# A hybrid attention layer on one core: denominators spread through DRAM, gate products on GpSimd, more copies on ScalarE

## The chip, the cores and the metric

One Trainium2 chip, of which the kernel uses one core. The metric is the device time of one execution in microseconds (us); lower is better. The core has a matrix engine (TensorE, in the profile PE, its weight loads PEld), VectorE (DVE), ScalarE (ACT), GpSimd (POOL) and SyncE (SP), which only issues DMAs here.

## The reference, cut to what matters

A decoder layer over 2048 tokens of width 1024: `h = rmsnorm(x)`, one input projection, two token mixers side by side, their gated outputs concatenated, an output projection, and the residual added. The change touches the first mixer, eight heads of 64 columns. Each of its heads is a mixture of three dilated windows:

```python
for window, dilation in ((128, 1), (512, 4), (2048, 16)):
    o, m, den = dilated_pattern(q, k, v, rel_bias, window, dilation)
    outs.append(o); log_dens.append(m + jnp.log(den))
alpha = jax.nn.softmax(jnp.stack(log_dens, axis=0), axis=0)
o_a = jnp.sum(alpha[..., None] * jnp.stack(outs, axis=0), axis=0)
mixed = jnp.concatenate([o_a * jax.nn.silu(z_a), o_b * jax.nn.silu(z_b)], axis=-1)
```

The kernel takes one maximum per query over the three windows, adds the three unnormalised outputs, and multiplies once by one over the summed denominators and once by the gate. The second mixer is a latent attention with eight heads.

## The kernel before

The kernel runs in stages. Up to about 670 us it projects the input in tiles and stores q, k, v and the gates in DRAM. From 672 to about 1012 us it works on the eight dilated heads, from 1012 to about 1540 us on the eight latent heads, and after that on the output projection.

**A dilated head.** `seq_s` makes the scores of a head in 24 tiles: `s_tile` (L883) for windows 1 and 2, `s_tile3` (L910) for window 3, each a few matmuls into a PSUM tile `S`, which DVE reduces with the bias (L895, L919). Windows 2 and 3 read regrouped copies of q that POOL casts in `q_turn` (L826, L828) into four rotating buffers. `m_fwd` and `m_back` combine the maxima over the windows: DVE expands them against a constant (L926, L933), PE folds the result. `seq_p` then takes the exponentials on ACT (L1016), turns 128x128 blocks of probabilities on PE into a PSUM tile `T` of three buffers (L1027, L1031), copies `T` to SBUF (`a_evac`, L1040 on DVE or L1042 on ACT, chosen by the tuple `EVA`, here two of four on each), multiplies with v (L1054, L1065) and adds up `acc` (L1076 on ACT, L1080 on DVE). The scores of head h+1 are woven into the second part of head h.

**The tail of a head.** `tail(h)` is woven into the next head's `seq_p`, one item every second step. `a_shift` moves the lower half of `acc` to 64 partitions by a DMA into `bot` (L1107) and loads the gate `g` (L1109). `a_den0` to `a_den2` sum the denominators to `rden`, 128 queries by 16 blocks, and take the reciprocal (L1102). The outputs lie the other way, 64 columns on partitions and 2048 queries along them, so the reciprocals must lie along the free axis, the same on all 64 partitions. `a_out` gets this by PE: four transposes of one broadcast column each into a `T` tile (L1116). Then `a_out2`, one step later, multiplies the gate with it on DVE (L1124), adds the two halves of the output (L1126, on POOL, in the last head on DVE), and multiplies by the gate on POOL (L1127). Four such rounds `m` make a head, 512 queries each; `a_store` writes `bot` to `mixD` (L1130).

**The latent heads** do the same thing another way (`b_den1`, `b_out`): PE turns a [128,4] tile of reciprocals once (L1397), DVE copies it to SBUF (L1399), SP writes it to the DRAM tile `rD` (L1401) and reads it back on 64 partitions with a source stride of 0 (L1403); POOL multiplies (L1418, L1419). `rD` has 16 entries, of which the latent heads use 8 to 15.

**What sets the order.** The program is traced in the order of the Python code, and a planner arranges each engine's instructions ahead of the run by its own model of their times; what it puts on one engine's queue is then executed in that order, each instruction waiting for its semaphores. In the latent stage alone PE's order is as written. All loads and most stores of both attention stages are issued by SP, also one queue in order. After the last dilated head, `tail(7)` is woven with the first score blocks of the latent heads (`b_blocks_s(0, 1)`), whose reductions (L1341) and copies (L1364) run on DVE; the first turned block of the latent stage is partly cleared by POOL (L1368) before the first product with its v (L1379).

Of the kernel before, what the change touches and what calls it, by code (L numbers as in the profile page):

```python
# [21 lines left out]
F32 = mybir.dt.float32  # L22
# [3 lines left out]
OP = mybir.AluOpType  # L26
# [25 lines left out]
NPA = 6  # L52
WPL = (1,)
MXB = 10
EVA = (0, 0, 1, 1)
EVB = (0, 1)
SCALE_B = 96.0 ** -0.5
QA0, KA0, VA0, ZA0, CQ0, CKV0, KR0, ZB0 = 0, 512, 1024, 1536, 2048, 2304, 2432, 2464
# [39 lines left out]
def hybrid_kernel(ctx: ExitStack, tc: tile.TileContext, x, positions, rel_bias, norm_gain, w_in,  # L98
                  a_q_gain, a_k_gain, q_c_gain, w_uq, kv_c_gain, w_ukv, qn_gain, qr_gain,
                  kn_gain, kr_gain, w_out, cmat, ctri, conehot, cinv, out, dbg=None):  # L100
    nc = tc.nc
    pe, dve, act, pool, sp = nc.tensor, nc.vector, nc.scalar, nc.gpsimd, nc.sync
# [26 lines left out]
    rD = [dr.tile([16, 128], F32, name=f"rD{i}") for i in range(16)]  # L129
# [3 lines left out]
    ident = CM[:, 0:128]  # L133
# [543 lines left out]
    for gi, (half, nm) in enumerate(seq):  # L677
# [18 lines left out]
        for i, unit in enumerate(units):  # L696
# [8 lines left out]
            if nm == "g0" and half == 1:  # L705
                b = 12 + i
# [46 lines left out]
            if nm == "g1":  # L753
                b = 8 * half + i
                todo_bg += [("q", b, clock[0]), ("k", b, clock[0] + 4)]
            credit = min(credit + RATE[half] * (1.5 if nm[0] == "z" else 1.0), 1.5)
            if credit >= 1 and todo_bg and todo_bg[0][2] <= clock[0]:
                credit -= 1
                kind, b, _ = todo_bg.pop(0)
# [8 lines left out]
    while todo_bg:  # L768
        kind, b, _ = todo_bg.pop(0)
# [33 lines left out]
    psS = pool_of("pss", "left", PSUM)  # L803
    PA2 = psO = None
    HD = [dict() for _ in range(8)]
# [298 lines left out]
    def a_shift(h):  # L1104
# [3 lines left out]
        H["g"] = PA2.tile([64, S], F32, name="gA_", bufs=1)  # L1108
        sp.dma_start(H["g"], GD[h // 2][64 * (h % 2):64 * (h % 2) + 64, :])  # L1109

    def a_out(h, m):
        H = HD[h]
        s = slice(512 * m, 512 * m + 512)
        tp = psS.tile([128, 4, 128], F32, name="T", bufs=3)
        for i in range(4):
            pe.transpose(tp[:, i, :], H["rden"][:, 4 * m + i:4 * m + i + 1].to_broadcast([128, 128]), ident)  # L1116
        H["tp", "out"] = tp

    def a_out2(h, m):
        H = HD[h]  # L1120
        s = slice(512 * m, 512 * m + 512)
        tp = H["tp", "out"]
        g = H["g"][:, s]
        dve.tensor_tensor(g, tp[0:64].rearrange("p a b -> p (a b)"), g, op=OP.mult)  # L1124
        o = H["bot"][:, s]
        (dve if h == 7 else pool).tensor_tensor(o, H["acc"][0:64, s], o, op=OP.add)  # L1126
        pool.tensor_tensor(o, o, g, op=OP.mult)  # L1127

    def a_store(h):
        sp.dma_start(mixD[h], HD[h]["bot"])  # L1130
# [64 lines left out]

    def tail(h):
        out = [lambda: (a_shift(h), a_den0(h)), lambda: a_den1(h), lambda: a_den2(h)]
        for m in range(5):
            out.append(lambda m=m: (a_out2(h, m - 1) if m else None, a_out(h, m) if m < 4 else None))
        return out + [idle, lambda: a_store(h)]  # L1200

    def lead(h, n):
        fs = seq_s(h)
# [15 lines left out]
    PA2 = pool_of("pa2", "right")  # L1219
# [337 lines left out]
    for b in range(4, 16):  # L1557
        c, o = divmod(b, 4)
# [67 lines left out]
```

## Time and profile before

| | us |
|---|---|
| median of 3 runs | 1735.38 |
| the three runs | 1735.31, 1738.95, 1735.38 |
| the profiled execution | 1730.76 |
| its span, first to last instruction | 1728.9 |

The profiled execution is another one than the three, 4.62 us below their median, and 1.86 us of it lie outside the span. "Busy" is the time in which an engine had an instruction running; matmuls are pipelined, so that their lengths overlap, and the start of the next instruction tells more of what one costs than its length. In a list of groups "idle" is the time in which the engine stood still just before the group's instructions, with what it waited for behind the arrow. A stretch is given in us from the span's start. An average over the span hides that the stages have different limits; the table by stretch below separates them.

### The profile page before, as it was taken

How to read it: one execution, taken by the hardware profiler on the slowest of the kernel's cores; microseconds unless marked ns; L12 is line 12 of the kernel's file. 1: busy time of each engine (PE TensorE's matmuls, PEld its weight loads, DVE VectorE, ACT ScalarE, POOL GpSimd, SP SyncE). 2: the span in 40 equal slices, each digit the busy share in tenths (PEclk: the TensorE clock that was granted, in tenths of full speed). 3: DMA queues.
4: the chain of work that ended last, by engine and by line, in shares of the span. 5: the costliest groups of instructions: out<-in, count | busy, mean ns of one | idle time of the engine just before them, and what ended most of it. 6: DMA issues, size and time to landing. Idle time of an engine off the chain costs nothing.

```text
span 1728.9 us, 29212 instructions
## 1 busy us (share of the span) xinstructions
PE 1650.1 (95%) x10118; PEld 1305.3 (75%) x10118; DVE 990.1 (57%) x2965; ACT 830.0 (48%) x2231; POOL 661.2 (38%) x671
## 2 busy tenths in 40 slices
PE   6999999989999889989999989999999999999998
PEld 5999899889999778777777665566565566557887
DVE  4655555155676134578888776666666666624331
ACT  5655545166566214267777735555555555520000
POOL 2454343016575011054444768266266251311000
PEclk9999999999999989989999999999999999999999
DMA  7356544542556575468774551231231220227642
GB/s 161 90 150 163 143 133 132 186 117 70 130 138 181 182 185 138 110 140 190 183 172 119 133 111 61 60 83 34 56 83 42 48 65 25 71 61 180 187 132 69
DMA packets 222600, 203.76 MB, mean 118 GB/s; under 512 B 102317, under 2 KB 188985, under 8 KB 216308
## 3 DMA queue, kind: packets, MB, share of 16 engines
q1 hardware_dynamic: 136852, 153.85, 35.3%
q10 hardware_dynamic: 85600, 48.04, 10.1%
q8 instruction: 80, 1.31, 0.3%
q14 instruction: 68, 0.56, 0.1%
HBM read 136.45 MB, written 72.20 MB: 121 GB/s over the span
## 4 chain that ended last, share of the span: by engine, by line
PE 75%; DMA 10%; DVE 6%; ACT 4%; issue 2%; POOL 2%; SPq 1%; ACTq 0%; DVEq 0%; POOLq 0%
PE O L1379 8%; PE T L1361 7%; PE mz L229 5%; PE mz L227 5%; PE mz L228 5%; PE O L1065 4%; PE S L883 3%; PE T L1027 3%; PE S L1336 3%; PE S L1338 3%; PE S L1337 3%; PE po L227 3%; PE po L229 3%; PE po L228 3%; PE S L910 2%; PE mm L229 2%
## 5 line engine op out<-in xcount | busy, mean ns | idle before, releaser
L1379 PE MATMUL O<-ptB,VB 128*64 128x512 f32 (+3 forms) x640 | 176.2, 560 | 19.7 <-ACT ptB L1366 18.4
L227 PE MATMUL mz<-wh,hTh 128*128 128x256 f32 (+2 forms) x600 | 182.6, 305 | 0.9 <-ACT hTh L221 0.7
L229 PE MATMUL mz<-wh,hTl 128*128 128x256 f32 (+2 forms) x600 | 178.4, 297 | 2.0 <-DVE hTl L222 2.0
L228 PE MATMUL mz<-wl,hTh 128*128 128x256 f32 (+2 forms) x600 | 177.8, 296 | 0.0
L1364 DVE COPY ptB<-T 128x512 f32<-128x512 f32 (+3 forms) x160 | 97.6, 610 | 126.6 <-PE T L1361 119.8
L1354 ACT ACTIVATE P<-P,msB 128x1024 f32<-128x1024 f32 (+4 forms) x104 | 109.7, 1055 | 125.5 <-DVE msB L1341 124.6
L270 DVE SCALAR_TENSOR_TENSOR wl<-wraw,ng,wh 128x256 fp32r<-128x256 f32 (+2 forms) x176 | 83.5, 512 | 113.6 <-ACT wh L269 110.9
L1336 PE MATMUL S<-kBh,qBh 96*128 96x512 f32 (+2 forms) x320 | 131.0, 409 | 5.5 <-DVE msB L1341 5.4
L1366 ACT ACTIVATE ptB<-T 128x512 f32<-128x512 f32 (+3 forms) x160 | 84.2, 526 | 108.0 <-PE T L1361 107.4
L1361 PEld LDWEIGHTS T<-CM,P 128*128 128x128 f32 x740 | 81.4, 143 | 69.2 <-issue 67.9
L227 PEld LDWEIGHTS mz<-wh,hTh 128*128 128x128 f32 x600 | 115.4, 192 | 3.2 <-ACT hTh L221 2.0
L229 PEld LDWEIGHTS mz<-wh,hTl 128*128 128x128 f32 x600 | 115.4, 192 | 2.7 <-DVE hTl L222 2.7
L1337 PE MATMUL S<-kBl,qBh 96*128 96x512 f32 (+2 forms) x320 | 116.8, 365 | 0.0
L1338 PE MATMUL S<-kBh,qBl 96*128 96x512 f32 (+2 forms) x320 | 116.7, 366 | 0.0
L228 PEld LDWEIGHTS mz<-wl,hTh 128*128 128x128 f32 x600 | 115.6, 193 | 0.1
L143 POOL TENSOR_TENSOR pst<-pst,CM 128x8 f32<-128x8 f32 x48 | 80.2, 1684 | 81.4 <-DVE pst L594 72.8
L269 ACT ACTIVATE wh<-wraw,ng 128x256 fp32r<-128x256 f32 (+2 forms) x168 | 76.6, 514 | 64.0 <-DMA wraw<-in_w_in_dram 26.0
L1361 PE MATMUL T<-CM,P 128*128 128x128 f32 x740 | 105.4, 285 | 0.0
L227 PE MATMUL po<-woh,mh 128*128 128x512 f32 x256 | 101.4, 397 | 1.6 <-ACT woh L1242 1.0
L228 PE MATMUL po<-wol,mh 128*128 128x512 f32 x256 | 101.0, 395 | 1.9 <-POOL wol L1243 1.9
L229 PE MATMUL po<-woh,ml 128*128 128x512 f32 x256 | 101.0, 395 | 0.0
L1379 PEld LDWEIGHTS O<-ptB,VB 128*64 128x64 f32 x640 | 38.8, 135 | 77.5 <-ACT ptB L1366 33.1
(489 smaller groups left out, 4607.8 us busy)
## 6 DMA issues: line engine op xcount, KB each, us to landing
wraw<-in_w_in_dram SPq DMA_DIRECT2D x72, 256.0 KB
V<-vA SPq DMA_DIRECT2D x24, 512.0 KB
xt<-in_x_dram SPq DMA_DIRECT2D x16, 512.0 KB
GD<-zst ACTq DMA_DIRECT2D x32, 256.0 KB
vA<-vA SPq DMA_DIRECT2D x8, 1024.0 KB
Q<-qT SPq DMA_DIRECT2D x8, 1024.0 KB
KH<-kT SPq DMA_DIRECT2D x16, 512.0 KB
KL<-kT SPq DMA_DIRECT2D x16, 512.0 KB
```

The costliest lines, as they stand in the source:

```text
L227: pe.matmul(ps, lh, rh, start=first, stop=False)
L228: pe.matmul(ps, lh, rl, start=False, stop=False)
L229: pe.matmul(ps, ll, rh, start=False, stop=last)
L270: dve.scalar_tensor_tensor(WL[key][:, k, :w], r[:, j, :w], ng[:, k:k + 1], f32(wh), op0=OP.mult, op1=OP.subtract)
L1336: pe.matmul(ps[:, :nm], H["q", "h"][:, q], H["k", "h"][:, k], start=True, stop=False)
L1337: pe.matmul(ps[:, :nm], H["q", "h"][:, q], H["k", "l"][:, k], start=False, stop=False)
L1338: pe.matmul(ps[:, :nm], H["q", "l"][:, q], H["k", "h"][:, k], start=False, stop=True)
L1354: act.activation(t, t, AF.Exp, bias=b, scale=-1.0, accum_out=H["den", c][:, i, d:d + 1])
L1361: pe.transpose(tp[:, d, :], p_part(h, c, d, 128 * j, 128), ident)
L1364: dve.tensor_copy(pt[:, d0:, :], tp[:, d0:, :])
L1366: act.activation(pt[:, d0:, :], tp[:, d0:, :], AF.Copy)
L1379: pe.matmul(o[64 * e:64 * e + 64, d0:, :], V[:, j + e, :], pt[:, d0:, :], start=(j == 0), stop=(j == 4 * c + 2), skip_group_check=True)
```

## The change

The tuple `EVA` goes from two of four copies on ACT to three of four. `a_rd0` turns the whole [128,16] tile of reciprocals with one transpose, copies the [16,128] result to SBUF on DVE, and writes it to `rD[h]` in DRAM. `a_rd1` reads 512 of these values back on 64 partitions into `rbA`, which has one buffer; the read for round m+1 is issued behind round m. `a_out` is now all of a round: the sum of the halves, the gate times `rbA` on POOL, and the product of both on POOL. `a_out2` goes, and the tail has nine items instead of ten.

```diff
-EVA = (0, 0, 1, 1)
+EVA = (0, 0, 0, 1)
...
+    def a_rd0(h):
+
+        tp = psS.tile([128, 4, 128], F32, name="T", bufs=3)
+        pe.transpose(tp[0:16, 0, :], HD[h]["rden"], ident)
+        rt = PA2.tile([16, 128], F32, name="rtA", bufs=1)
+        dve.tensor_copy(rt, tp[0:16, 0, :])
+        sp.dma_start(rD[h], rt)
+
+    def a_rd1(h, m):
+
+        rb = HD[h]["rb", m] = PA2.tile([64, 512], F32, name="rbA", bufs=1)
+        dst = rD[h][4 * m:4 * m + 4, :]
+        sp.dma_start(rb, bass.AP(tensor=dst.tensor, offset=dst.offset, ap=[[0, 64], [1, 512]]))
+
     def a_out(h, m):
         H = HD[h]
         s = slice(512 * m, 512 * m + 512)
-        tp = psS.tile([128, 4, 128], F32, name="T", bufs=3)
-        for i in range(4):
-            pe.transpose(tp[:, i, :], H["rden"][:, 4 * m + i:4 * m + i + 1].to_broadcast([128, 128]), ident)
-        H["tp", "out"] = tp
-
-    def a_out2(h, m):
-        H = HD[h]
-        s = slice(512 * m, 512 * m + 512)
-        tp = H["tp", "out"]
-        g = H["g"][:, s]
-        dve.tensor_tensor(g, tp[0:64].rearrange("p a b -> p (a b)"), g, op=OP.mult)
-        o = H["bot"][:, s]
+        o, g = H["bot"][:, s], H["g"][:, s]
         (dve if h == 7 else pool).tensor_tensor(o, H["acc"][0:64, s], o, op=OP.add)
+        pool.tensor_tensor(g, H["rb", m], g, op=OP.mult)
         pool.tensor_tensor(o, o, g, op=OP.mult)
+        if m < 3:
+            a_rd1(h, m + 1)
...
     def tail(h):
         out = [lambda: (a_shift(h), a_den0(h)), lambda: a_den1(h), lambda: a_den2(h)]
-        for m in range(5):
-            out.append(lambda m=m: (a_out2(h, m - 1) if m else None, a_out(h, m) if m < 4 else None))
-        return out + [idle, lambda: a_store(h)]
+        out.append(lambda: (a_rd0(h), a_rd1(h, 0)))
+        for m in range(4):
+            out.append(lambda m=m: a_out(h, m))
+        return out + [lambda: a_store(h)]
```

## Rows read from the trace of the kernel before

**Rows 1.** The page, part 1: busy time of each engine.
```profile
PE 1650.1 (95%) x10118; PEld 1305.3 (75%) x10118; DVE 990.1 (57%) x2965; ACT 830.0 (48%) x2231; POOL 661.2 (38%) x671
```

**Rows 2.** Busy time by stretch: stage of heads, parts of it, its end.
```profile
core 0: us, PE busy (x) PEld busy (x) DVE busy (x) ACT busy (x) POOL busy (x), PEclk, DMA share, GB/s
744.00:1012.00 268.00, 260.20 (x2052) 200.60 (x2052) 215.12 (x876) 188.49 (x661) 138.12 (x144) 0.99 0.68 153
820.00:838.00 18.00, 18.00 (x147) 14.15 (x146) 15.22 (x74) 18.00 (x67) 2.87 (x5) 1.00 0.81 175
838.00:844.00 6.00, 6.00 (x49) 5.12 (x49) 5.87 (x29) 0.75 (x3) 6.00 (x6) 1.00 0.60 221
...
1012.00:1020.00 8.00, 2.51 (x10) 1.60 (x9) 7.34 (x14) 0.81 (x1) 6.38 (x6) 0.80 0.00 0
```

**Rows 3.** PE in order of time, inside one head (start, length, instruction).
```profile
835.78 0.60 PE L1116 MATMUL T<-CM,rden 128*128 128x128 f32 x4
836.22 0.60 PE L1027 MATMUL T<-CM,Pr 128*128 128x128 f32 x4
```

**Rows 4.** Instructions of L1116 (ns min/median/max, first and last start).
```profile
L1116 PE MATMUL T<-CM,rden x128: 270/273/421, 755.6 to 1012.1; 128*128 128x128 f32 x128
```

**Rows 5.** L1399, which copies turned denominators in the latent heads.
```profile
L1399 DVE COPY rtB<-T x31: 247/269/273, 1026.3 to 1502.3; 4x128 f32<-4x128 f32 x31
```

**Rows 6.** Copies out of PSUM tile T, by engine.
```profile
L1040 DVE COPY PT<-T x80: 539/678/693, 701.7 to 1001.0; 128x512 f32<-128x512 f32 x56, 128x384 f32<-128x384 f32 x24
L1042 ACT ACTIVATE PT<-T x80: 468/592/609, 702.2 to 1002.2; 128x512 f32<-128x512 f32 x64, 128x384 f32<-128x384 f32 x16
```

**Rows 7.** Groups by line and shape, 744 to 1012 (busy, mean, idle).
```profile
L1126 POOL TENSOR_TENSOR bot<-acc,bot 64x512 f32<-64x512 f32 x28 | 34.8, 1271 | 10.6 <-DMA bot<-acc 9.7 <-DVE gA__10110 L1124 0.9
...
L926 DVE TENSOR_TENSOR E<-mc,CM 128x128 f32<-128x128 f32 x6 | 6.8, 1135 | 0.2
...
L1124 DVE TENSOR_TENSOR gA__10110<-T,gA__10110 64x512 f32<-64x512 f32 x4 | 2.7, 678 | 0.5 <-PE T L1116 0.5
...
L926 DVE TENSOR_TENSOR E<-m,CM 128x128 f32<-128x128 f32 x6 | 1.7, 291 | 0.7 <-PE S L1091 0.5
```

**Rows 8.** Who waited for whom, 744 to 1012 (us, times, longest).
```profile
POOL Q L826 <- PE S L883: 61.2, 11, 11.1
...
POOL bot L1126 <- DMA bot<-acc: 9.7, 3, 7.7
...
PE S L910 <- POOL Q L828: 4.0, 1, 4.0
...
PE T L1027 <- DVE PT L1040: 2.6, 3, 1.6
```

**Rows 9.** SP in order of time, through one head's tail.
```profile
855.39 0.54 SPq L1130 DMA_DIRECT2D mixD<-bot  x1
...
869.45 0.50 SPq L1107 DMA_DIRECT2D bot<-acc  x1
```

**Rows 10.** SP in the latent stage: a wait group, one pair in time.
```profile
SPq L1403 <- DMA rD<-rtB: 46.3, 27, 5.2
...
1110.33 0.25 SPq L1401 DMA_DIRECT2D rD<-rtB  x1
1111.56 0.45 SPq L1403 DMA_DIRECT2D rbB<-rD  x1
```

**Rows 11.** The stage's end in order of time: DVE, PE, POOL.
```profile
1012.81 4.62 DVE L1126 TENSOR_TENSOR bot<-acc,bot 64x512 f32<-64x512 f32 x4 [0.39 <-issue]
...
1017.44 0.65 DVE L1124 TENSOR_TENSOR gA__12563<-T,gA__12563 64x512 f32<-64x512 f32 x1
...
1018.81 0.80 PE L1336 MATMUL S<-kBh,qBh 96*128 96x512 f32 x1 [5.38 <-DVE msB L1341]
...
1024.46 1.08 PE L1379 MATMUL O<-ptB,VB 128*64 128x512 f32 x4
...
1019.74 0.20 POOL L1368 MEMSET ptB<- 128x128 f32 x1
```

## The prediction

> **What bounds the kernel now.** I began with the busy times of the whole span [rows 1]: PE works 95% of it, DVE 57%, ACT 48%, POOL 38%. That is an average over stages, so the second view is the table by stretch [rows 2], over the stretch in which the tails of the dilated heads lie. There PE is busy 260.2 of 268 us, DVE 215.1, ACT 188.5, POOL 138.1. Inside one head the picture shifts: from 820 to 838 us ACT has no gap at all (18.00 of 18), while POOL works 2.87 us; from 838 to 844 us, where the tail runs, ACT is nearly free (0.75 of 6), DVE full (5.87) and POOL full. PE is full in both. So PE sets the length of a head, and an edit is worth what it takes from PE, as long as nobody else becomes late. The third view is who waited for whom [rows 8]: PE waited 2.6 us for a copy of `T` by DVE (three times) and 4.0 us, once, for a cast of q by POOL; POOL itself waits long for PE (61.2 us for L826 alone). The last view is the stage's end in order of time [rows 11]: PE stands still for 5.38 us because DVE, in order, is held by the additions of `tail(7)`.
>
> Below, 0.2%, 3.5 us, is about what a measurement of this kernel can tell from no change.
>
> **The change part by part.**
>
> *Transposes off PE.* L1116 has 128 instructions [rows 4], 16 per head in four groups. The next group starts 0.44 us after the start of one [rows 3]; this, not the length of 0.60 us, is what a group takes. The tails of heads 0 to 6 lie in a full PE: 7 x 4 x 0.44 = 12.3 us go. Each of those tails gets one transpose back, a quarter of a group by the same rows: 7 x 0.11 = 0.8 us. Net: **-11.5 us**. This is the main term. `tail(7)` lies where PE stands still anyway; its four groups count nothing.
>
> *Gate product off DVE.* Per head four L1124 of 0.68 us [rows 7] leave DVE, 2.7 us of a head, and a copy of [16,128] comes, 0.27 us by the nearest row [rows 5]. DVE is no bound of a head on average, and PE's work covers it: 0. At the stage's end it is on the path: of the L1124 there the last, 0.65 us, lies between the additions and the reduction that frees PE [rows 11]. The others lie before the additions, which wait for the load of `bot`. The additions take 4.62 us, 1.16 each, against 0.68 for an instruction of that size on DVE [rows 7]; POOL's products run beside them. With `rbA` two DMAs away, POOL is idle for part of that time, and of the 1.9 us in excess I take half. Together **-1.6 us**, between 0 and the whole of PE's 5.4 us.
>
> *Product on POOL.* 32 products at 1.27 us [rows 7], 40.6 us, 5.1 per head, beside 138.1 busy of 268 [rows 2]. POOL would then be at some 65%, with gaps as the wait of 61.2 us shows [rows 8]: 0 on the path from the work itself. The Trainium skill, in "GPSIMD Engine Reference", section 4.1, "Engine selection", speaks against this move: it wants elementwise work on VectorE and gives GpSimd as about two times slower. The rows agree, 1.27 against 0.68; by the rule alone the product would cost 32 x 0.59 = 19 us more engine time, and that is time of the kernel only where POOL is late.
>
> *Contention of POOL and DVE.* L926 on DVE takes 0.29 us in one place and 1.14 on average in another, where POOL is at work [rows 7]. Four expansions a head on DVE (L926, L933), seven heads: 28 instructions, and POOL is busy for 15% more of the time. 28 x 0.15 x 0.85, the excess, would be 3.6 us on DVE; the chain of the maxima is partly under PE's other work, so I take **+1.0 us**, with 0 below and 28 x 0.85 = 24 us above if all of them met a product and none was covered. The Trainium skill, in "SBUF — State Buffer", section "Who interferes with whom", says that a DVE instruction with two SBUF inputs waits out a whole GpSimd instruction that reads SBUF, and one with a single SBUF input does not; by it L1124, which read PSUM, hindered nobody, and its successor on POOL does. The trace shows the first half, with these numbers.
>
> *Copies to ACT.* Of the 160 copies [rows 6], 40 change sides: 5 per head, 0.59 us each on ACT. From 838 us on, ACT has room. In the full stretch (820 to 838) lie the 12 copies of windows 2 and 3, of which three more go to ACT, 1.8 us per head. PE's waits for DVE's copies, 2.6 us [rows 8], could go; waits for ACT's could come. Cover: the exponentials are done some time before their blocks are turned. I take 0, with ends -2.6 and 7 x 1.8 = +12.4 us.
>
> *The round trip.* SP issues 8 writes and 32 reads more, and rather than stand free it now waits: for the copy by DVE, for the write to land, for each round of POOL. Behind it are queued the loads of q, k, bias and v for the next heads. No row shows a read of `rbA`; the nearest are those of the latent heads, where the read follows the write by 1.23 us [rows 10], the longest wait being 5.2. A round is then 1.2 to 5.2 us for the read plus 1.27 for the product on POOL before the buffer is free: 10 to 26 us for the four of a head. Before, `bot` is stored at 855.39 and needed again at 869.45 [rows 9]: 14 us of room in a period of about 38. I take 0: v, k and q are loaded ahead. At worst the later store holds the next tail, which only delays work that PE doesn't wait for. At the stage's end, POOL clears a block (L1368, 1019.74) that PE's first product needs at 1024.46 [rows 11]. If it stands behind the rounds of `tail(7)`, these end between some 1021 and 1034 us, so PE loses 0 to 10 us; the clearing needs none of their results, so I take 0.
>
> Sum: -11.5 - 1.6 + 1.0 = -12.1 us. The profiled execution took 1730.76 us, which gives 1718.7; it lies 4.6 us below the median of the runs, and against that, 1735.38, the time is 1723.3. I give the latter.
>
> **The rivals.**
>
> *PE's small waits go too.* DVE gets 2.7 us per head from the gate products and about 3 from copies, so PE's waits for it (2.6 us) vanish, as does most of the 5.4 us at the stage's end: -12.1 - 2.6 - 3.8 = -18.5, 1716.9 us. For it: DVE is full just where the tail lies. Against: the waits are few, and ACT must take over without new ones.
>
> *ACT becomes the bound.* It is full for 18 us of a head already, and three more copies there lengthen this by 1.8 us. If the next head's blocks are then turned as fast as their exponentials come, the head doesn't get shorter: -12.1 + 12.4, 1735.7 us, no change. It decides once the exponentials end later than PE asks for them. Against: behind the full stretch ACT has a hole of over 5 us.
>
> *POOL's queue turns a wait for DRAM into a wait of PE (slower).* The trace has one case: POOL stood in order for 7.7 us before the load of `bot`, a cast of q was queued behind, and PE lost 4.0 us [rows 8]. After the change POOL has four more such waits in each tail. If in each of seven tails one cast stands behind a product that waits for `rbA`, 7 x 4.0 = 28 us come: -12.1 + 28 = +15.9, 1751.3 us. It decides where the rounds reach into the time at which the next casts are due. For it: DMA share is 0.81 from 820 to 838 us [rows 2], so reads queue. Against: the casts of the other tails run well ahead of PE, and POOL waits for PE more than the reverse.
>
> **How the numbers follow.** Forecast (1719 to 1730): 0.58. All waits go: 0.14. ACT: 0.12, no change. POOL: 0.16, slower. So faster 0.72, same 0.12, slower 0.16. The likeliest is 1723.3. The range reaches down to 1711, past 1716.9 by what the rest of the stage's end could give, and up to 1737, past the case of ACT; it leaves out POOL's case and small tails, 0.2.
>
> **What would show it.** In the new profile L1116 is gone, with eight transposes of [128,16] in its place; PE is still over 95% busy between 776 and 960 us, and the period of a head is about 1.6 us shorter. DVE falls by some 48 us over the stage, ACT rises by 23, POOL by 41. PE's waits for POOL (L828) and ACT (L1042) stay under 5 us each in the stage, and the gap at the stage's end is under 5 us. The prediction is wrong if PE waits for L1042 or L826/L828 in every head, or if the gap between the stages grows because L1368 or a load stands behind the rounds of `tail(7)`.

## The result, and the profile after

The changed kernel takes **1784.84 us** (median of 4 runs, 1780.87 to 1787.33) against 1735.35 of the kernel before, measured beside it (4 runs): the ratio is 1.028 with a 95% interval of 1.0255 to 1.0305. It is 49 us slower, where 12 us faster was forecast and 1711 to 1737 given as the range. Lines behind the change move: the sum of the halves is L1129 now, the gate product L1130, the last product L1131, the store L1136, the write of `rD` L1117, its read L1123; in the latent stage the score matmuls are L1343 to L1345, the reduction L1348, the copies L1371 and L1373, the product with v L1386.

Part 1 of the page answers to [rows 1], and the table by stretch to [rows 2] (first three lines), with four stretches of 96 us behind:

```profile
PE 1652.2 (93%) x9998; PEld 1308.2 (73%) x9998; DVE 948.0 (53%) x2901; ACT 849.4 (48%) x2271; POOL 700.1 (39%) x703
```

```profile
core 0: us, PE busy (x) PEld busy (x) DVE busy (x) ACT busy (x) POOL busy (x), PEclk, DMA share, GB/s
744.00:1012.00 268.00, 238.93 (x1821) 188.17 (x1822) 177.23 (x817) 200.52 (x699) 145.60 (x152) 0.94 0.68 150
820.00:838.00 18.00, 18.00 (x148) 13.85 (x147) 13.80 (x75) 18.00 (x68) 9.45 (x10) 1.00 1.06 196
838.00:844.00 6.00, 6.00 (x50) 5.13 (x49) 5.01 (x25) 3.76 (x11) 5.92 (x8) 1.00 0.51 116
768.00:864.00 96.00, 93.25 (x739) 72.31 (x739) 70.78 (x322) 71.13 (x246) 48.65 (x57) 0.98 0.80 173
864.00:960.00 96.00, 85.69 (x658) 68.67 (x657) 66.95 (x335) 70.34 (x248) 47.92 (x52) 0.95 0.54 124
960.00:1056.00 96.00, 74.25 (x511) 52.48 (x510) 40.20 (x122) 54.28 (x155) 65.15 (x56) 0.88 0.55 125
1056.00:1152.00 96.00, 69.92 (x347) 41.87 (x344) 48.16 (x123) 35.72 (x73) 71.84 (x55) 0.86 0.42 99
```

The same four stretches of the kernel before:

```profile
768.00:864.00 96.00, 95.80 (x772) 73.35 (x774) 80.45 (x335) 67.73 (x243) 43.54 (x52) 1.00 0.80 177
864.00:960.00 96.00, 95.86 (x771) 75.35 (x766) 82.18 (x364) 67.22 (x236) 48.59 (x53) 1.00 0.60 138
960.00:1056.00 96.00, 86.42 (x568) 58.61 (x568) 64.71 (x162) 55.97 (x158) 67.38 (x54) 0.96 0.52 119
1056.00:1152.00 96.00, 92.88 (x511) 57.89 (x511) 62.19 (x171) 51.39 (x109) 56.40 (x44) 1.00 0.19 53
```

Over the whole span the other engines moved nearly as forecast (DVE -42, ACT +19, POOL +39 us). PE, expected over 95% busy from 776 to 960 us, was busy for 170.9 of 184 (93%). In these four stretches PE's busy time fell from 370.96 to 323.11 us, so it stands still 48 us more, of the 54 by which the two profiled executions differ. Its busy time over the whole span didn't fall with the work (1650.1 before, 1652.2 now, with 120 matmuls fewer), while its mean granted clock fell from 0.984 to 0.964. Who keeps PE waiting (PE's waits, 744 to 1012 us and 1012 to 1130 us):

```profile
PE O L1065 <- ACT acc L1076: 16.8, 4, 7.6
PE S L972 <- DVE E L926: 4.9, 4, 1.9
PE S L910 <- POOL Q L828: 4.1, 1, 4.1
...
PE S L1343 <- DVE msB L1348: 13.7, 2, 12.9
PE O L1065 <- ACT acc L1076: 7.7, 1, 7.7
PE S L1345 <- POOL qBl L1303: 6.0, 1, 6.0
PE O L1386 <- ACT ptB L1373: 5.8, 1, 5.8
```

The wait that the rivals feared, for POOL's casts (L828), is what it was, 4.1 against 4.0 us [rows 8]. New are waits for the sums `acc` on ACT, and a block of waits in the first latent head. Both lead to the tails, the sums in part (below, under why the prediction was wrong). The last store of a dilated head falls at 1086.6 us, 66.8 us later than before; its row of the changed kernel:

```profile
L1136 SPq DMA_DIRECT2D mixD<-bot x8: 460/464/2455, 808.5 to 1086.6; - x8
```

The first five stores are at 808.5, 867.5, 918.9, 960.1 and 1008.0 us, on average 50 us apart, while a head of PE takes 37. A tail no longer fits into a head, so each ends later against its head than the one before: the first store comes 31 us later than in the kernel before (777.3), the fifth 83 us (924.9). SP's and POOL's timelines show where `tail(1)` spends its time:

```profile
815.55 0.49 SPq L1107 DMA_DIRECT2D bot<-acc  x1
816.14 0.54 SPq L844 DMA_DIRECT2D V<-vA  x1
816.73 12.02 SPq L817 DMA_DIRECT2D KL<-kT  x1
828.84 0.55 SPq L1123 DMA_DIRECT2D rbA<-rD  x1
...
857.62 0.53 SPq L1123 DMA_DIRECT2D rbA<-rD  x1
867.07 0.38 SPq L844 DMA_DIRECT2D V<-vA  x1
867.54 2.46 SPq L1136 DMA_DIRECT2D mixD<-bot  x1
870.04 0.60 SPq L1109 DMA_DIRECT2D gA__10096<-GD  x1
870.74 1.92 SPq L844 DMA_DIRECT2D V<-vA  x1
874.09 2.89 SPq L1107 DMA_DIRECT2D bot<-acc  x1
```

```profile
829.70 5.04 POOL L1129 TENSOR_TENSOR bot<-acc,bot 64x512 f32<-64x512 f32 x4 [7.25 <-DMA bot<-acc]
836.04 1.28 POOL L1130 TENSOR_TENSOR gA__9556<-rbA,gA__9556 64x512 f32<-64x512 f32 x1 [1.30 <-DMA rbA<-rD]
...
858.35 1.27 POOL L1131 TENSOR_TENSOR bot<-bot,gA__9556 64x512 f32<-64x512 f32 x1
...
877.69 1.28 POOL L1130 TENSOR_TENSOR gA__10096<-rbA,gA__10096 64x512 f32<-64x512 f32 x1 [2.96 <-DMA gA__10096<-GD]
```

A read of 512 values waits on SP behind a load of `KL` that took SP 12.02 us; the last product ends at 859.62 and its store is issued 8 us later, behind a load of v that waits 8.9 us for PE; and since `bot` and the gate have one buffer each, the gate of the next tail is loaded only behind that store, and the next tail's first product runs at 877.69, 10 us after it. In the five tails of the heads' stage 2.8 to 20.1 us pass between the issue of a read and the start of the product that uses it (19 of 20 above 4.5, median 8); POOL's other work and the load of the gate are in it. In the three tails of the latent stage the first read of a tail takes 8.8 to 12.8 us, the third and fourth 2.8 to 3.1.

Three tails are then still to be done in the latent stage. There DVE, in order, waits for `bot` of the last one, does its additions, and only then the reductions that PE needs; SP issues the latent heads' first gate load at 1087.42, behind the last store. DVE and PE of the changed kernel:

```profile
1072.32 4.62 DVE L1129 TENSOR_TENSOR bot<-acc,bot 64x512 f32<-64x512 f32 x4 [7.65 <-DMA bot<-acc]
...
1077.53 0.58 PE L1343 MATMUL S<-kBh,qBh 96*128 96x256 f32 x1 [12.89 <-DVE msB L1348]
```

This is the gap of 5.38 us of [rows 11] again, now 12.89.

For the experiments the time is cut at three marks of each profiled execution: the first and the eighth maximum of the heads (`mc`, L961) and the first and last product of the latent stage (L1386). "Heads" runs from the first to the eighth maximum, "end" from there to the first latent product, "latent" over the latent products. One execution of a kernel differs from another by a few us in these columns.

| kernel | median us | ratio (95%) | heads | end | latent | last store |
|---|---|---|---|---|---|---|
| before | 1735.35 | 1 | 290.9 | 61.3 | 516.5 | 1019.8 |
| the change | 1784.84 | 1.0280 (1.0255-1.0305) | 289.5 | 75.4 | 551.7 | 1086.6 |
| copies alone | 1731.47 | 0.9981 (0.9963-0.9999) | 285.6 | 58.7 | 521.0 | 1025.9 |
| trip alone | 1762.10 | 1.0156 (1.0124-1.0187) | 277.5 | 67.0 | 554.2 | 1069.3 |
| one read a tail | 1740.38 | 1.0030 (1.0008-1.0051) | 288.5 | 55.9 | 529.5 | 1033.9 |
| control: 19 panels | 1735.79 | 1.0005 (0.9986-1.0025) | 289.3 | 60.5 | 516.0 | 1023.3 |
| halves | 1737.25 | 1.0007 (0.9988-1.0027) | 286.9 | 54.8 | 531.1 | 1041.9 |
| both links cut | 1740.29 | 1.0028 (1.0013-1.0043) | 291.4 | 58.9 | 521.8 | 1037.4 |
| reads from POOL | 1802.73 | 1.0384 (1.0356-1.0413) | 292.2 | 81.9 | 562.0 | 1104.9 |

### The profile page after: what moved, and what is told of

It is laid out like the page before. It is cut to its first block, busy times and chain, and to the rows that moved or that the text cites. A ratio compares the mean times of both kernels' runs of the same rounds, so it can differ in the third digit from the quotient of the medians.

```text
span 1783.1 us, 29024 instructions
## 1 busy us (share of the span) xinstructions
PE 1652.2 (93%) x9998; PEld 1308.2 (73%) x9998; DVE 948.0 (53%) x2901; ACT 849.4 (48%) x2271; POOL 700.1 (39%) x703
## 3 DMA queue, kind: packets, MB, share of 16 engines
q1 hardware_dynamic: 139668, 158.12, 35.8%
## 4 chain that ended last, share of the span: by engine, by line
PE 73%; DMA 12%; ACT 6%; DVE 4%; POOL 2%; issue 2%; SPq 1%; DVEq 0%; ACTq 0%; POOLq 0%
PE O L1386 8%; PE T L1368 7%; PE mz L229 6%; PE mz L227 6%; PE mz L228 6%; PE O L1065 3%; PE po L227 3%; PE po L228 3%; PE po L229 3%; PE S L1345 3%; PE S L1343 3%; PE S L1344 3%; PE T L1027 2%; PE mm L229 2%; PE mm L227 2%; PE mm L228 2%
## 5 line engine op out<-in xcount | busy, mean ns | idle before, releaser
L1386 PE MATMUL O<-ptB,VB 128*64 128x512 f32 (+3 forms) x640 | 179.7, 567 | 25.8 <-ACT ptB L1373 21.8
L1371 DVE COPY ptB<-T 128x512 f32<-128x512 f32 (+3 forms) x160 | 97.6, 610 | 134.2 <-PE T L1368 125.4
L1343 PE MATMUL S<-kBh,qBh 96*128 96x512 f32 (+2 forms) x320 | 131.7, 413 | 13.7 <-DVE msB L1348 13.7
L1373 ACT ACTIVATE ptB<-T 128x512 f32<-128x512 f32 (+3 forms) x160 | 84.2, 526 | 119.7 <-PE T L1368 119.1
L1345 PE MATMUL S<-kBh,qBl 96*128 96x512 f32 (+2 forms) x320 | 117.1, 367 | 6.0 <-POOL qBl L1303 6.0
L1065 PE MATMUL O<-PT,V 128*64 128x256 f32 (+1 forms) x560 | 83.3, 391 | 24.5 <-ACT acc L1076 24.5
L1386 PEld LDWEIGHTS O<-ptB,VB 128*64 128x64 f32 x640 | 39.1, 136 | 85.2 <-ACT ptB L1373 35.3
```

The costliest lines, as they stand in the source:

```text
L1065: pe.matmul(o[half, 128 * q:128 * (q + k)], V[:, kb, :], pt[:, i:i + k, :], start=(u == 0), stop=(w == 1 and u == 1), skip_group_check=True)
L1343: pe.matmul(ps[:, :nm], H["q", "h"][:, q], H["k", "h"][:, k], start=True, stop=False)
L1345: pe.matmul(ps[:, :nm], H["q", "l"][:, q], H["k", "h"][:, k], start=False, stop=True)
L1371: dve.tensor_copy(pt[:, d0:, :], tp[:, d0:, :])
L1373: act.activation(pt[:, d0:, :], tp[:, d0:, :], AF.Copy)
L1386: pe.matmul(o[64 * e:64 * e + 64, d0:, :], V[:, j + e, :], pt[:, d0:, :], start=(j == 0), stop=(j == 4 * c + 2), skip_group_check=True)
```

## Experiments: which part loses the time

**The copies alone**, in the kernel before.

```diff
-EVA = (0, 0, 1, 1)
+EVA = (0, 0, 0, 1)
```

> The kernel before with the copies alone moved: three of four on ACT, the tail as it was. Theory (the four rounds of a tail, one after the other through one buffer and SP's queue, last longer than a head): the copies have little part in the loss of 49 us, so 1725 to 1745 us. Rival A (copies on ACT hold PE): 1765 us or more.

Measured 1731.47 us, 0.9981 (0.9963 to 0.9999). The copies have no loss of their own; as the only cause, ACT is out.

**The trip alone.** The changed kernel with the copies as before.

```diff
-EVA = (0, 0, 0, 1)
+EVA = (0, 0, 1, 1)
```

> The changed kernel with the copies put back, two of four on each engine. Theory: the loss stays, 1770 to 1795 us, and the stores of the tails fall behind by more than a head as in the changed kernel. Rival A (copies on ACT): back to 1715 to 1740 us.

Measured 1762.1 us, below the range expected: the trip alone costs 27 us and the copies, worth -3 without it, add 22 on top of it. That they add up was wrong. With the copies on ACT, its queue is full where `acc` is due: from 976 to 982 us of the changed kernel ACT works 6.00 of 6 us while PE waits for its L1076, 7.58 us in one piece:

```profile
976.00:982.00 6.00, 0.00 (x0) 0.00 (x0) 0.00 (x0) 6.00 (x27) 6.00 (x5) 0.63 0.64 165
982.50 3.68 PE L1065 MATMUL O<-PT,V 128*64 128x256 f32 x20 [7.58 <-ACT acc L1076]
```

With the trip alone the heads' stage got 13 us shorter than before the change (277.5); the loss lies behind it, where three tails are left over (stores at 1018.1, 1045.2 and 1069.3).

## Experiments: what makes a tail long

**One read a tail** in place of four, 2048 values into 8 KB a partition; to make room, 19 panels of `P` instead of 21. All products stay on POOL. With all 21 panels there is no room (44 KB a partition wanted for a pool of buffers, 39.6 left), so there is no time for that. The control is the kernel before with 19 panels.

```diff
-        rb = HD[h]["rb", m] = PA2.tile([64, 512], F32, name="rbA", bufs=1)
+        rb = HD[h]["rb"] = PA2.tile([64, S], F32, name="rbA", bufs=1)
...
-        if m < 3:
-            a_rd1(h, m + 1)
```

> The changed kernel with one read of all 2048 reciprocals per tail (8 KB buffer, paid for with 19 instead of 21 probability buffers), products on GpSimd and copies as changed. Theory (the rounds of a tail wait for one another, tails last 51 us on average where a head lasts 37, and those left over run in the latent stage): stores of the tails again one head apart, the last before 1040 us, and a time 5 to 20 us under the control. Rival B (products on GpSimd): 30 us or more over the control.

> A control for the next run: the kernel before with 19 instead of 21 rotating buffers for blocks of probabilities (8 KB of SBUF less). 1733 to 1755 us by any theory.

Measured 1740.38 us, the control 1735.79. Some 44 of the 49 us come back with all of POOL's products in place, so the products as such are not the cause; nor is the volume read, which is the same (eight reads of 512 KB for 32 of 128 KB). The row of its gate products in the second tail shows the difference: the first at 809.3, the fourth at 813.0 us, one behind the other, where the changed kernel has 818.1 and 852.5:

```profile
L1130 POOL TENSOR_TENSOR gA__9550<-rbA,gA__9550 x4: 1267/1270/1323, 809.3 to 813.0; 64x512 f32<-64x512 f32 x4
```

Tails are a head apart again (stores at 789.4, 828.7, 862.4, 899.5). The theory had it 5 to 20 us below the control; it lies 5 above. Two waits are left at the stage's end, DVE's additions waiting 4.26 us at 1025.34 and PE 7.2 us behind them.

**Halves.** `bot`, the gate and `rbA` of odd heads lie on partitions 64 to 127 of the same tiles, so two tails can be under way; four reads stay.

```diff
+        a, z = (0, 64) if h % 2 == 0 else (64, 0)
+        H["bot"], H["g"] = HALF["bot"][a:a + 64, :], HALF["g"][a:a + 64, :]
+        sp.dma_start(H["bot"], H["acc"][z:z + 64, :])
```

> The changed kernel with the output halves, the gate and the spread reciprocals of even heads on partitions 0 to 63 and of odd heads on 64 to 127 of shared tiles, so that a tail's loads of bot and g needn't wait for the store of the tail before; the four rounds stay one after the other. Theory: of the 51 us per tail the 8 to 10 between a store and the next tail's first product go, the rounds stay at about 40, so the backlog shrinks to some 3 us per head: 1735 to 1760 us. If the link from store to next tail were all of it: 1715 to 1730 us. If it had no part: 1775 us or more.

Measured 1737.25 us. The link from a store to the next tail's loads, cut alone, brings back some 47 us. The rounds and the link are thus not two sums that add: either one, taken away, lets the tails keep up with the heads (here from the third on: 907.5, 942.9, 974.7), and a tail that keeps up costs little. Both kernels are new plans of all engines; plans of nearly equal work stood up to 14 us apart here (below), and 44 and 47 us lie well beyond that.

**Reads from POOL's queue** instead of SP's.

```diff
-        sp.dma_start(rb, bass.AP(tensor=dst.tensor, offset=dst.offset, ap=[[0, 64], [1, 512]]))
+        pool.dma_start(rb, bass.AP(tensor=dst.tensor, offset=dst.offset, ap=[[0, 64], [1, 512]]))
```

> The changed kernel with the four reads of a tail issued by POOL in place of SP; nothing else moves. Theory (a tail is slow because its reads stand in SP's order behind loads that wait, and because bot and g have one buffer): the time from issue to product falls from a median of about 8 us to 3 to 4 us, the tails come 35 to 45 us apart in place of 51, and the time falls to 1745 to 1770 us; what is left is the link from a tail's store to the next tail's loads. Rival C (POOL's queue turns the wait for the read into waits of what stands behind it, so that the place of the issue doesn't matter): POOL still stands still for each read and the time stays at 1775 to 1795. If the loss were the transport itself (a read of 128 KB under the other loads), the rounds stay at 5 to 20 us and the time within 1775 to 1795 too; the two differ in the duration of the read in the trace.

Measured 1802.73 us, 18 slower than the change and above every range. The theory was wrong in this: taking the reads out of SP's queue gains nothing. On POOL they are issued in order among casts of q that wait for PE (35.8 us from 744 to 1012 us, 25.4 in the change); the time from read to product stays at 2.8 to 15.5 us, of which the read itself, from issue to landing, takes 2.8 to 8.8.

**The last five heads by PE**, the first three through DRAM (`b_rden` and `b_out2` are `a_out` and `a_out2` of before).

```diff
+        if h >= 3:
+            for m in range(5):
+                out.append(lambda m=m: (b_out2(h, m - 1) if m else None, b_rden(h, m) if m < 4 else None))
+            return out + [idle, lambda: a_store(h)]
```

> The changed kernel with the denominators of heads 3 to 7 spread by PE's transposes and DVE's product as before, of heads 0 to 2 through DRAM; copies as changed. Theory (only what is left over at the end of the heads costs time): the later tails, 20 us each, catch up, the last store comes before 1040 us, and the time is 1722 to 1737 us. Rival D (each tail through DRAM costs a share of its own, 53 us over the copies-alone kernel divided by eight): 3 x 6.6 = 20 us over 1731, so 1751 us.

Measured 1755.2 us, far from the theory and near rival D's 1751, but not as a share for each tail: the delay of three tails is paid where the way changes. The gate of head 3 is loaded behind the late store of head 2 (899.7), and PE waits 13.2 us for DVE, which waits for it. The head in which this happens took 61 us.

**Product on DVE**, with one read.

```diff
-        pool.tensor_tensor(g, H["rb"][:, s], g, op=OP.mult)
+        dve.tensor_tensor(g, H["rb"][:, s], g, op=OP.mult)
```

> One read for a tail, as in the run of that name, with the gate product on DVE in place of POOL (32 products of 512 columns). It prices the third part of the change. The prediction took the product off DVE as worth 1.6 us at the end of the stage and on POOL as costing nothing. Theory: with one read the tails keep up, POOL gains 32 x 1.27 = 41 us of room and DVE loses about 32 x 0.65 = 21; neither bounds: within 6 us of 1740 either way. Rival B (GpSimd's slower product is what makes a tail late): 1715 to 1732. If DVE's order is what suffers, since its products would wait in order for the read: 1748 to 1765.

Measured 1751.8 us, 11 more than with the product on POOL: the heads' stage took 304.6 us, and PE waited 10.4 us in it for expansions on DVE (its L955 for L933). Here the product on POOL was the better place, although one takes 1.27 us there; as this is another plan, some of the 11 us may be the plan's.

**POOL's product cut**, with the order of the change held (the program after planning is left as it is, and 32 instructions are made smaller):

```diff
+            for i in blk.instructions:
+                if is_gp(i):
+                    i = copy.replace(i, ins=[short(p) for p in i.ins], outs=[short(i.outs[0])])
```

> The changed kernel with its order held; only its 32 gate products on POOL are cut from 512 columns to 8 (a part of the computation is left out). It prices the third part of the change on POOL. Theory (a tail's length is made of reads in SP's queue and of the link from store to loads; the product adds 1.27 us to each round, 5 us to a tail of 51 which comes once a head): of the 49 us lost 5 to 25 come back, 1760 to 1780. Rival B (the product on POOL is the cause): below 1750.

Measured 1767.87 us: 17 of the 49 us, for products cut from 1.27 to 0.20 us each, 34 us in all. While tails are the slow chain, half of the product's time counts; the last store comes 12.5 us earlier (1074.1).

## Experiments: what the removed work was worth

**Both links cut**, one read and halves. And one read without halves, with the **last head by PE** (the edit of the five heads with `h >= 7`).

> The changed kernel with both links cut: one read of 2048 columns for a tail, into a buffer of 8 KB a partition (19 panels of P in place of 21, which by itself was worth nothing), and bot, g and the read denominators of odd heads on partitions 64 to 127 of the same tiles, so that two tails can be under way. Theory (the backlog is made of the rounds and of the link from store to loads, nothing else): tails come one head apart (35 to 40 us), the last store falls at 1010 to 1030, and what TensorE gains by the missing transposes (about 11 to 14 us, by the run with one round of four) shows: 1715 to 1733 us. Rival E (the end of the stage has a wait of its own, DVE in order behind the last tail's loads, which neither link explains): 1735 to 1745, as either cut alone gave, with a gap of PE of 5 us or more at 1020 to 1035.

> One read for a tail, as in the run of that name, and the last head's denominators spread by TensorE as before the change (heads 0 to 6 go through DRAM). It tells what the end of the stage costs. Theory (of the 5 us that one read still loses, most lies where DVE waits in order for the last tail's loads): it helps little unless the loads come sooner, since bot of the last tail still waits for the store of the one before: 1733 to 1742. Rival F (the last tail's own trip through DRAM is what holds the end): without it 1720 to 1732.

Measured 1740.29 and 1739.14 us. The last head's trip isn't what costs the rest, and of both links cut the time is rival E's, but not its sign: PE's longest gap at the stage's end is 3.6 us. With no tail late, the gain of 11 us that the prediction rests on doesn't show. In the first, PE's busy time from 768 to 960 us is 183 of 192 us, in the kernel before 191.7, and its granted clock 0.98 against 1.00: the work is gone and the time isn't. So the main term itself had to be measured.

| kernel | median us | ratio (95%) | heads | end | latent |
|---|---|---|---|---|---|
| one round of four (planned anew) | 1724.44 | 0.9939 (0.9915-0.9964) | 293.5 | 45.9 | 520.8 |
| transposes left out (planned anew) | 1738.27 | 1.0020 (1.0001-1.0039) | 302.3 | 54.6 | 516.3 |
| transposes twice (planned anew) | 1742.92 | 1.0043 (1.0027-1.0059) | 302.1 | 56.4 | 515.8 |
| transposes cut, order held | 1735.26 | 0.9985 (0.9967-1.0003) | 288.7 | 62.2 | 517.5 |
| transposes and products cut, order held | 1730.37 | 0.9970 (0.9952-0.9988) | 288.1 | 60.8 | 520.4 |
| transposes twice, order held | 1743.92 | 1.0050 (1.0032-1.0068) | 299.3 | 62.7 | 520.9 |

**One round.** In the kernel before, transposes and gate products of rounds 1 to 3 are left out.

```diff
     def a_out(h, m):
...
+        if m:
+            return
...
-        dve.tensor_tensor(g, tp[0:64].rearrange("p a b -> p (a b)"), g, op=OP.mult)
+        if m == 0:
+            dve.tensor_tensor(g, tp[0:64].rearrange("p a b -> p (a b)"), g, op=OP.mult)
```

> The kernel before without the transposes and the gate product of three of four rounds in each tail; it leaves out the division by the denominators of three quarters of the dilated heads' queries. It measures what PE's transposes and DVE's products cost before. The prediction's term: 7 x 3 x 0.44 = 9.2 us from PE, perhaps 1 to 3 us more from DVE at the stage's end, so 1723 to 1727 us. Rival C (they lay beside other work): 1733 to 1738 us.

10.5 us less. It looked like a proof of the main term, but the heads' stage is not shorter (293.5); the gain lies at the end (45.9).

**Transposes left out**, products kept (the edit above, with a second line for the other rounds); and **transposes twice**.

```diff
+        else:
+            dve.tensor_tensor(g, H["acc"][0:64, s], g, op=OP.mult)
```

```diff
-        for i in range(4):
+        for i in [0, 1, 2, 3] * 2:
             pe.transpose(tp[:, i, :], H["rden"][:, 4 * m + i:4 * m + i + 1].to_broadcast([128, 128]), ident)
```

> The kernel before with the transposes of the denominators' rounds 1 to 3 left out (96 of 128); DVE multiplies g in those rounds by rows of acc instead, so that its products stay (a part of the computation is left out and another takes its place). It prices the prediction's main term alone. Prediction's step: 7 heads x 3 rounds x 0.44 = 9.2 us less, 1724 to 1728 us. Rival G (PE's work there isn't what sets the pace; the 10.5 us of the run with one round came from the products that it left out as well): 1731 to 1736.

> The kernel before with each group of four transposes of the denominators done twice into the same tile. It prices the main term upward. Prediction's step: 7 x 4 x 0.44 = 12.3 us more in the heads and up to 1.8 at the end, 1746 to 1750 us. Rival G: PE had room, 1735 to 1741.

Leaving out 96 transposes brought nothing (1738.27); doing them twice cost 7.5 us. But the planner sees other instructions and arranges all engines anew: in the first, POOL does four additions in one go (4.96 us), in front of a cast that PE needs, and DVE's products, which now read `acc`, took 0.68 to 1.48 us on average in a tail against 0.68. Work and order are mixed. The last three keep the order of the kernel before on every engine.

**Order held: transposes cut to 8 columns; products cut too; transposes twice.** After planning, instructions of L1116 are replaced by shorter ones, those of L1124 too (as above), or each of L1116 is followed by its twin:

```diff
+                if is_tr(i):
+                    i = copy.replace(i, ins=[short(i.ins[0], 8), short(i.ins[1], 8, 128)], outs=[short(i.outs[0])])
```

```diff
+                if is_tr(i):
+                    twin = copy.replace(i, name=f"I-{900000 + n}", sync_info=None)
```

> The kernel before with its planned order held on every engine; only, after the planning, each of the 128 transposes of denominators is cut from 128 columns to 8 (the products then take one value of each block for 128 queries, a part of the computation left out). Prediction's step: the groups cost 0.44 us each and most of that goes, at most 7 x 4 x 0.44 = 12.3 us, if a short one takes a third of a long one 8 us: 1723 to 1728. Rival G (PE's work isn't what sets the pace of a head): 1733 to 1737. The trace tells the mechanism: if PE gains gaps in 768 to 960 and its granted clock falls in some stretch behind one, what was saved is handed back there.

> As the run before it, and the 32 gate products on DVE are cut from 512 columns to 8 as well, at the same held order. It prices the removed half of the change (transposes and product) without what came in its place and without a new plan. Prediction's steps: 12.3 and 1.6 us less, 1721 to 1726. If the products matter more than the transposes (as the run with one round against the run without transposes says), 1716 to 1722. Rival G for both: 1733 to 1737.

> The kernel before with its order held and each of the 128 transposes of denominators issued twice in a row. Prediction's step: PE is full, so 7 x 4 x 0.44 = 12.3 us more, 1745 to 1750. Rival G: below 1739.

How much PE work changes is read as in [rows 3]. PE of the run with short ones: a group now takes 0.21 us in place of 0.44 (medians over all groups 0.25 and 0.45).

```profile
841.38 0.35 PE L1116 MATMUL T<-CM,rden 8*128 8x8 f32 x4
841.59 0.64 PE L1027 MATMUL T<-CM,Pr 128*128 128x128 f32 x4
```

Of the 28 groups in the heads' tails that is 28 x 0.22 = 6.2 us less, and the time fell by 2.6 us (0.0015 of it; interval 5.7 less to 0.5 more). Twice is 28 x 0.43 = 12 us more, and the time rose by 8.7 (5.6 to 11.8). With the products cut too, 5.2 us less (2.1 to 8.3). None of the three fell into the range of the prediction's step: the short ones alone lie in rival G's, the other two between the ranges. Work added to a full PE cost some 0.7 of its length (0.5 to 1.0), work removed gave some 0.4 (nothing to 0.9); whether the two differ isn't shown.

The run with short transposes tells where the rest of the 6.2 us went. From 744 to 1012 us PE's waits sum to 10.6 us against 7.4 before, 2.6 of them new ones for expansions on DVE, and the granted clock is 0.97 against 0.99 [rows 2]; with the transposes twice it stays at 0.99.

```profile
744.00:1012.00 268.00, 257.07 (x2044) 197.34 (x2041) 220.81 (x884) 189.47 (x675) 141.70 (x149) 0.97 0.69 155
```

The same work took DVE longer (220.8 us against 215.1). Three of the expansions L933, of 1.1 to 1.3 us before, took 2.6 to 3.0, while POOL worked on the tail, casts and bias; the group before and with short transposes:

```profile
L933 DVE TENSOR_TENSOR E<-m,CM 128x64 f32<-128x64 f32 x6 | 5.1, 854 | 0.3
L933 DVE TENSOR_TENSOR E<-m,CM 128x64 f32<-128x64 f32 x6 | 10.8, 1794 | 0.3
```

These are single executions, and which of the two, waits or clock, weighs more isn't separated.

**Both links cut, old copies**, the version meant to beat both kernels.

> Both links cut (one read a tail, halves of shared tiles), all products as in the change, and the copies of PT as before the change (two of four on ScalarE). Theory (the trip's gain on TensorE is real, and in the run with both links cut ScalarE, with three of four copies, held it back: PE waited for ACT's PT copies 9 times there in 768 to 960 where it waited for nothing before): the stretch from first to eighth maximum falls to 277 to 285 us, and the time to 1718 to 1731, below the kernel before. Rival G (that stretch is set by the order of the engines and not by PE's work, so that it stays at 287 to 293): 1735 to 1743, as with the new copies.

1749.32 us, with 298.2 us from first to eighth maximum, above all ranges. It missed on the other side: the copies on ACT, which cost 22 us beside late tails, are worth 9 where tails keep up. No version with the trip came below the kernel before; the copies alone are the best of the complete kernels that ran, by 0.2%, at the edge of what can be told.

## Why the prediction was wrong

**The step that failed: "The round trip ... I take 0"**, with its reason, "at worst the later store holds the next tail, which only delays work that PE doesn't wait for". Four rounds were put at 10 to 26 us against 14 us of room, so the upper bound already broke the room, and the bound was then not carried on. Three things were missed. The price of a round was taken from a wait in the latent stage [rows 10], where SP has room; in the heads' stage it was mostly 5 to 20 us from issue to use. The 1.2 to 5.2 us were added up for one tail, while a tail longer than a head delays the next, by some 13 us each time. And "work that PE doesn't wait for" holds only until `acc`, of which there are two buffers, comes round: ACT waited for POOL's additions, which read `acc`, and PE for ACT, as ACT's and PE's timelines of the changed kernel have it:

```profile
887.89 1.09 ACT L1076 ACTIVATE acc<-O 128x512 f32<-128x512 f32 x2 [4.41 <-POOL bot L1129]
888.54 1.74 PE L1065 MATMUL O<-PT,V 128*64 128x256 f32 x10 [2.55 <-ACT acc L1076]
```

This chain is shown for part of the loss. ACT's waits for POOL sum to 8.5 us (two waits), PE's for these sums to 24.5; before waits of 5.57 and 7.58 us, ACT had no gap and worked on exponentials. How late tails led to that isn't traced. That the late tails are the cause rests on the two cuts, one read and halves. By these two, the term that was put at 0 cost 44 to 47 us.

**Transposes off PE, -11.5.** Rows 3 and 4 give the work rightly: it left PE. But the sum took its whole length as time. At held order 6.2 us of it gave 2.6 (interval from nothing to 5.7); by that ratio 12.3 would give about 5, an estimate. A table that shows PE full tells that more work costs; less work gave PE new waits and a lower clock. ACT and DVE were 70% and 85% busy there, each with an order made for a slower PE.

**Gate product off DVE, -1.6.** At held order, transposes and products cut together gave 5.2 us against 2.6 for transposes alone; the difference is of the forecast's size but lies inside the intervals. With one read, the product on DVE cost 11 us more than on POOL, in another plan. The sign agrees with the runs; the size isn't shown.

**Product on POOL, 0.** Wrong as long as tails are late (17 us). With one read the whole change lies 5 us above the kernel before with all products on POOL, so there it can't cost much; no run prices it alone.

**Contention, +1.0.** DVE's expansions make four groups. Of the kernel before, two are in [rows 7] and one stands above with the short transposes; the fourth, and behind it the four of the changed kernel:

```profile
L933 DVE TENSOR_TENSOR E<-mc,CM 128x64 f32<-128x64 f32 x6 | 6.4, 1075 | 0.0
```

```profile
L926 DVE TENSOR_TENSOR E<-mc,CM 128x128 f32<-128x128 f32 x6 | 8.4, 1400 | 0.2
L933 DVE TENSOR_TENSOR E<-mc,CM 128x64 f32<-128x64 f32 x7 | 5.2, 737 | 0.0
L933 DVE TENSOR_TENSOR E<-m,CM 128x64 f32<-128x64 f32 x6 | 3.3, 555 | 0.5
L926 DVE TENSOR_TENSOR E<-m,CM 128x128 f32<-128x128 f32 x6 | 2.0, 328 | 0.8 <-PE S L1091 0.8
```

L926 on `mc` rose from 1135 to 1400 ns, but the four groups together fell from 20.0 to 18.9 us: the extra work that the term stands for didn't come. The long L926 of before (1.98 us at 851.84) ran beside POOL's L993, not beside a tail, so that POOL's busy share was a poor measure of how often the two meet. Two of the changed kernel's took 3.13 us, beside the end of a product (L1130), a cast and L993 in turn, so the meeting that was feared did occur, twice. PE's waits for L926 on DVE rose all the same (4.9 us against 1.9 over all heads).

**Copies, 0.** Alone -3 us, beside late tails +22; the term depends on the state of the tails, and the sum had no place for that.

**The end of the stage.** The zero for POOL's clearing of the first block was nearly right (PE waited 2.6 us for it); what came instead, 12.89 us, were the additions of `tail(7)`, which stand in DVE's order and wait for a load that waits for a store. The prediction had named this, a gap that grows because a load stands behind the rounds, as a sign of being wrong.

**The rivals.** Slower had 0.16, by POOL's casts. That mechanism had the side right and the place wrong: PE's wait for casts didn't change, and the delay reached it through a buffer, ACT's order, and the next stage. That slower came is no success of this rival.

Open: how much of the main term is there to be had under a plan made for it. Two plans of nearly the same work (one round; transposes left out, which keeps 24 products on DVE) stood 14 us apart, more than the term.

## What to carry to other kernels

A chain off the critical path must be measured against its period: sum all its waits, at the prices of the stage in which it runs, and if the sum is longer than the period, the difference adds up over the iterations until a buffer with few copies or the next stage brings it to the bound engine. Where it fitted again, by one read in place of four or by a second buffer, its cost was nearly gone, and both together brought no more. Work taken from a full engine can be worth less than its length (here about 0.4, from nothing to 0.9), and where a planner arranges the order, price it at held order first.

## What was not expected of the hardware

In these traces PE's granted clock falls behind some of PE's own gaps. In the kernel before the granted clock is 1.00 from 768 to 960 us, with PE busy for 191.66 of 192 us. With transposes left out, it is 0.98 and 0.96 in the two halves, and the table in stretches of 2 us of that run shows where:

```profile
806.00:808.00 2.00, 0.66 (x4) 0.42 (x4) 1.40 (x2) 1.47 (x4) 2.00 (x3) 1.00 0.01 4
808.00:810.00 2.00, 0.76 (x5) 0.76 (x6) 0.00 (x0) 0.00 (x0) 2.00 (x4) 0.95 0.00 0
810.00:812.00 2.00, 2.00 (x11) 1.40 (x12) 1.02 (x8) 0.00 (x0) 2.00 (x2) 0.50 0.59 156
812.00:814.00 2.00, 2.00 (x17) 1.27 (x15) 0.00 (x0) 0.60 (x1) 2.00 (x3) 0.70 0.86 360
814.00:816.00 2.00, 2.00 (x21) 1.83 (x21) 1.28 (x3) 0.60 (x1) 1.26 (x2) 1.00 0.13 35
```

PE stood still for 2.6 of 4 us (2.25 of it waiting for a cast by POOL), and soon after work came it ran at the lower level, 1.2 GHz, for some 3 us: the matmuls of L910 start 0.13 us apart at 809.5 and 0.22 apart at 810.2. Such a gap is longer than it looks. Not every gap does this: in the kernel before PE works 0.46 us from 976 to 978 and the clock stays at 1.00. In the four stretches of the changed kernel the clock was 0.98, 0.95, 0.88 and 0.86, part of it while PE had nothing to do.

A transpose of 8x8 in place of 128x128 still took half the time: 0.058 us from start to start inside a group, where the long one takes 0.109 (medians; a group of four 0.21 against 0.44).
